# Stepping the mixer's side jobs at every eighth weight tile, not every fourth, with up to six convolution steps a visit

## The chip, the cores and the metric

The kernel runs on one core of a Trainium2 chip. Its engines are TensorE (PE), VectorE (DVE), ScalarE (ACT), GpSimd (POOL) and SyncE (SP), which here issues the transfers. Each engine executes its own list of instructions in order and waits on semaphores for the others. The metric is the device time of one execution in microseconds.

## The reference

One inference step of a two-layer decoder, for a prompt of 256 tokens and eight samples of four tokens each: 288 columns in all, 1024 features. A layer, cut to what matters:

```python
x = x + 0.5 * swiglu(rmsnorm(x, g_ffn1), w_ffn1_up, w_ffn1_down)
u = rmsnorm(x, g_mix)
x_pool, qkv, z, a, b, glu_in, gates = split(u @ w_in)
o_pool = multiscale_pool(st_pool, x_pool)                    # branch "pool"
o_dn = gated_deltanet(st_dnconv, st_dn, qkv, z, a, b)        # branch "dn"
o_cm = conformer_conv(st_cm, glu_in)                         # branch "cm": causal convolution of width 31
br = einsum('blnc,ncd->blnd', stack([o_pool, o_dn, o_cm]), w_branch)
merged = sum(sigmoid(gates) * br)
x = x + merged @ w_out
x = x + 0.5 * swiglu(rmsnorm(x, g_ffn2), w_ffn2_up, w_ffn2_down)
x = x + sigmoid(rmsnorm(x, g_ple) @ w_ple_gate) * (p[i] @ w_ple_proj)
```

The outputs are x after a last RMSNorm, and the new states of the three branches.

## The kernel before

Activations lie with the features on the 128 partitions and the 288 columns along the free axis. All large products go through one stream of weight tiles of 128x128, 1716 tiles a layer, in the order of `tile_order` (line 54). Eight tiles make a unit of 512 KB, which SP loads (`raw`); ACT rounds it to `hi` and DVE forms the rest `lo` (`prep`, line 302), two units ahead of use (`AHEAD`). A tile costs three matmuls of 288 columns (`mm3`): hi by the rounded activations, hi by their rest, lo by the rounded. `gemm` (line 331) walks over the tiles of one output; its results lie in `m` tiles in PSUM, those of side matmuls in `a` tiles.

A layer's stages, by weight tile: feed-forward 1 (0 to 527), the mixer (528 to 1107), feed-forward 2 (1108 to 1635), the embedding (1636 to 1715). The mixer's products come in the order k, glu, q, v, pool, z (528 to 751), a first gate and four `pool_w` tiles (752 to 763), gates and branch product of "pool" (to 851), the gates of "dn" (852 to 915) and "cm" (916 to 979), the branch product of "cm" (980 to 1011) and of "dn" (1012 to 1043), and `w_out` (1044 to 1107).

What the branches compute beside these products is cut into steps of generators, the side jobs: `pre` (logits, decays and norms of the delta rule), `conv` (short convolution of q, k, v), `gp` (the delta rule of the prompt: inverses, values, states, 40 steps, with `finish` for each half of it, which norms and gates the output and rounds it into `oh` and `ol`), `pool` (pooling, 4 steps), `gs` (the delta rule of the samples, 26 steps, the last eight of which multiply a mask into a 96x512 tile, run one wide matmul and update four 128x128 states), and `cm` (the width-31 convolution, 77 steps). A step issues work on DVE, ACT and PE; jobs wait for each other by flags (`gp` for `pre`'s `ready`, `gs` for an inverse of `gp`).

After every `HOOK`-th weight tile `gemm` calls the hook. In the mixer and behind it that is `pump` (line 1081). It reckons with planned costs: `te.t` is what PE was given since the last visit, `v.t` what DVE was given, and `owed` their difference, saved up to 1.5 (`CARRY`):

```python
for s in list(sides):
    for _ in range(LIMS[s[0]]):
        if self.v.t >= self.te.t + owed[0] or not step(s):
            break
```

The jobs are visited in the order pre, conv, gp, pool, gs, cm (`ORDER`), each up to its number in `LIMS`. Where a branch's result must be there, the program calls `until` (line 1089), which steps the named jobs until it is, with no weight tiles between: `get_pool` ahead of tile 760, `get_cm` ahead of 980, `get_dn` ahead of 1012 (it wants all three `finish` of the delta rule done; it names conv, pre, gp and gs).

The recorded program is then ordered by a scheduler that can shift instructions a little where their inputs are thought to be late; the order on each engine is fixed before the run.

Of the kernel before, what the change touches and what calls it, by code (L numbers as in the profile page):

```python
# [155 lines left out]
MF = (7, 4)  # L156
MP = (6, 6)
WARM = 16
HOOK = 4
WB = 3  # L160
A00 = 0
CAHEAD = 2
CTAPS = range(3, 31, 3)
DMIN = 0.0
ORDER = ("pre", "conv", "gp", "pool", "gs", "cm")
LIMS = (1, 1, 1, 1, 1, 3)


def pause(n):
# [57 lines left out]
class Net:  # L227
# [103 lines left out]
    def gemm(self, xs, nk, nout=1, spare=False, mid=None):  # L331
        pss = [self.aps()[:, :N] if spare else self.mps() for _ in range(nout)]
        for k in range(nk):
            xh, xl = xs(k)
            for ps in pss:
                self.mm3(ps, xh, xl, k == 0, k == nk - 1)
                self.tick += 1
                if self.hook and self.tick % HOOK == 0:
                    self.hook()
# [722 lines left out]
    def mix(self, l):  # L1062
# [11 lines left out]
        def step(s):  # L1074
            try:
                return next(s[1]) != "wait"
            except StopIteration:
                sides.remove(s)
                return False

        def pump():
            owed[0] = min(owed[0] + self.te.t - self.v.t, CARRY)
            self.v.t = self.te.t = 0.0
# [3 lines that stand above are left out]
# [431 lines left out]
```

## Time and profile before

| what | before |
|---|---|
| median of 3 runs | 1501.1 us (1499.58 to 3540.52) |
| profiled execution | 1498.33 us |
| its span | 1496.5 us |
| PE busy | 1482.9 us, 99% |
| DVE busy | 1077.9 us, 72% |
| ACT busy | 787.1 us, 53% |
| DMA | 250.03 MB, mean 167 GB/s |

The span is from the first to the last instruction of the program on the core. PE is busy nearly throughout; what matters is what it is busy with, and whether a stage takes more than its weight tiles need.

### The profile page before, as it was taken

The page shows a single profiled execution, that of the slowest core. Times are in us where ns is not written, and L with a number is a line of the kernel's source. Part 1 is how long each engine was busy: PE and PEld are TensorE (multiplying, and loading weights), DVE is VectorE, ACT ScalarE, POOL GpSimd, SP SyncE. Part 2 cuts the span into 40 slices and gives each one's busy share as a digit, 9 for nine tenths or more (in the row PEclk, how much of TensorE's full clock was granted, in tenths as well). Part 3 has the DMA queues.
Part 4 walks back from the last instruction along what each step waited for, and adds up shares of the span by engine and source line. Part 5 has one row for each costly group of instructions (what it writes and reads, how often), then busy time and mean ns, then how long its engine had stood idle before and what let it go on. Part 6 is the DMA issues. An engine that isn't in the chain of part 4 may idle for free.

```text
span 1496.5 us, 30281 instructions
## 1 busy us (share of the span) xinstructions
PE 1482.9 (99%) x12280; PEld 1464.2 (98%) x12280; DVE 1077.9 (72%) x2045; ACT 787.1 (53%) x1410; POOL 9.0 (1%) x34
## 2 busy tenths in 40 slices
PE   9999999999999999999999999999999999999997
PEld 9999999999999999999999999999989999999997
DVE  6575559998889655555867655699987986556556
ACT  6444446865664544443544444479557554444444
POOL 0000000000000000000000000000000000000000
PEclk9999999999999999999999999999999999999999
DMA  7555564655365555555555555555544755555552
GB/s 253 184 160 166 169 183 153 160 165 184 110 207 184 161 165 169 169 167 167 157 165 177 166 169 161 182 163 154 170 157 128 228 170 158 169 161 173 169 159 71
DMA packets 84572, 250.03 MB, mean 167 GB/s; under 512 B 19760, under 2 KB 24240, under 8 KB 84432
## 3 DMA queue, kind: packets, MB, share of 16 engines
q1 hardware_dynamic: 84000, 247.70, 53.9%
q8 instruction: 96, 1.57, 0.4%
q10 hardware_dynamic: 432, 0.40, 0.1%
q14 instruction: 44, 0.36, 0.1%
HBM read 239.52 MB, written 8.54 MB: 166 GB/s over the span
## 4 chain that ended last, share of the span: by engine, by line
PE 92%; ACT 4%; DVE 3%; issue 1%; DMA 0%; SPq 0%; DVEq 0%
PE m L205 84%; PE a L205 8%; ACT hi L310 1%; DVE lo L205 1%; DVE w L205 1%; ACT L568 0%; ACT w L716 0%; DMA x<-in_x 0%; DVE rsq L205 0%; ACT w L561 0%; ACT big L568 0%; ACT big L465 0%; DVE big L205 0%; ACT w L516 0%; ACT L701 0%
## 5 line engine op out<-in xcount | busy, mean ns | idle before, releaser
L205 PE MATMUL m<-big,hi 128*128 128x288 f32 x4008 | 803.0, 296 | 0.1
L205 DVE TENSOR_TENSOR lo<-raw,hi 128x1024 fp32r<-128x1024 f32 (+1 forms) x431 | 524.6, 1218 | 258.6 <-ACT hi L310 256.8
L310 ACT ACTIVATE hi<-raw 128x1024 fp32r<-128x1024 f32 (+1 forms) x431 | 456.3, 1059 | 452.3 <-PE m L205 274.4
L205 PEld LDWEIGHTS m<-big,hi 128*128 128x128 f32 x4008 | 643.1, 188 | 0.8 <-ACT big L346 0.3
L205 PE MATMUL m<-big,lo 128*128 128x288 f32 x2004 | 591.2, 295 | 0.0
L205 PE MATMUL m<-act,hi 128*128 128x288 f32 x2688 | 546.0, 298 | 0.6 <-ACT hi L310 0.6
L205 PEld LDWEIGHTS m<-act,hi 128*128 128x128 f32 x2688 | 430.4, 188 | 2.9 <-issue 1.2
L205 PE MATMUL m<-act,lo 128*128 128x288 f32 x1344 | 396.5, 296 | 0.5 <-DVE lo L205 0.3
L205 PEld LDWEIGHTS m<-big,lo 128*128 128x128 f32 x2004 | 377.2, 188 | 0.0
L205 PEld LDWEIGHTS m<-act,lo 128*128 128x128 f32 x1344 | 252.5, 188 | 1.8 <-DVE lo L205 1.5
L205 DVE TENSOR_TENSOR ar<-m,rsb 128x288 f32<-128x288 f32 x130 | 59.0, 454 | 47.1 <-PE m L205 43.5
L346 ACT ACTIVATE big<-h 128x288 fp32r<-128x288 f32 x96 | 41.8, 436 | 60.4 <-DVE h L205 60.4
L439 ACT ACTIVATE s<-ar 128x288 f32<-128x288 f32 x88 | 38.2, 436 | 65.5 <-DVE ar L205 65.4
L205 DVE SCALAR_TENSOR_TENSOR big<-big,par,big 128x256 f32<-128x256 f32 x160 | 70.8, 477 | 0.6
L205 DVE TENSOR_TENSOR big<-h,big 128x288 fp32r<-128x288 f32 x96 | 43.5, 454 | 19.5 <-ACT big L346 19.4
L205 DVE TENSOR_TENSOR h<-s,m 128x288 f32<-128x288 f32 x84 | 37.8, 450 | 19.3 <-ACT s L439 19.3
L371 ACT ACTIVATE sq<-x 128x288 f32<-128x288 f32 x62 | 26.9, 437 | 36.7 <-DVE x L205 36.4
L205 DVE TENSOR_TENSOR acc<-acc,sq 128x288 f32<-128x288 f32 x68 | 30.8, 454 | 11.4 <-ACT sq L371 10.9
L516 ACT ACTIVATE w<-big,par 128x256 f32<-128x256 f32 x80 | 37.2, 514 | 0.2
L205 DVE SCALAR_TENSOR_TENSOR w<-big,par,w 128x312 f32<-128x312 f32 x72 | 34.4, 533 | 2.8 <-ACT w L561 2.6
L205 DVE TENSOR_TENSOR big<-big,w 128x512 f32<-128x512 f32 x40 | 27.3, 683 | 5.6 <-ACT w L516 5.2
L205 PE MATMUL a<-w,big 32*32 32x32 f32 (+3 forms) x480 | 27.4, 223 | 0.3
(222 smaller groups left out, 893.8 us busy)
## 6 DMA issues: line engine op xcount, KB each, us to landing
raw<-in_w SPq DMA_DIRECT2D x427, 512.0 KB, 3.5
big<-in_dn_in SPq DMA_DIRECT2D x16, 512.0 KB, 5.5
out_dn_s<-big SPq DMA_DIRECT2D x8, 512.0 KB, 3.5
x<-in_x SPq DMA_DIRECT2D x4, 288.0 KB, 4.9
big<-in_cm_in SPq DMA_DIRECT2D x2, 544.0 KB, 4.6
big<-in_cm_in SPq DMA_DIRECT2D x4, 272.0 KB, 4.9
out_cm_s<-big SPq DMA_DIRECT2D x4, 272.0 KB, 4.6
raw<-in_w SPq DMA_DIRECT2D x4, 256.0 KB, 5.1
```

Source lines behind the costliest of these rows:

```text
L205: return f(*a, **k)
L310: nc.scalar.activation(hi[:, a:b], src[:, a:b], AF.Copy)
L346: nc.scalar.activation(hi, src, AF.Copy, scale=1.0 if scale is None else scale)
L371: nc.scalar.activation(s, src, AF.Square)
L439: nc.scalar.activation(s, ar, AF.Silu)
L516: nc.scalar.activation(ahead[nxt][:, i], ext[j][:, nxt:nxt + NP], AF.Copy, scale=wj(j, nxt))
```

## The change

Two constants: the hook is called after every eighth weight tile, and `cm` may take up to six steps at a visit. The other jobs keep one step a visit, and `CARRY` stays 1.5.

```diff
-HOOK = 4
+HOOK = 8
...
-LIMS = (1, 1, 1, 1, 1, 3)
+LIMS = (1, 1, 1, 1, 1, 6)
```

No instruction is added or removed on PE, DVE, POOL and SP; ACT gets 17 table loads and not 13. What moves is the order. Three places follow.

PE in layer 0 at the start of the `dn` branch product (tile 1012). `m_934` and `m_882` are the last tiles of the `cm` branch product, `m_939` and `m_937` the first of `dn`; `big_825` and `big_889` are `oh`. Before:

```order
L205 MATMUL m_934_5994<-big_803_5286,hi_922_5921 128x288
L205 MATMUL m_934_5994<-big_804_5287,hi_922_5921 128x288
L205 MATMUL m_934_5994<-big_803_5286,lo_923_5922 128x288
L205 MATMUL m_939_6016<-big_825_5388,hi_922_5921 128x288
L205 MATMUL m_943_6036<-big_825_5388,hi_929_5959 128x288
```

And in the changed kernel, where the `a` rows of 128x512 belong to the samples' state updates (`gs`) and the others to `gp` and to the samples' `finish` (its transpose is `a_888`):

```order
L205 MATMUL m_882_5786<-big_790_5192,lo_867_5693 128x288
L205 MATMUL a_886_5805<-w2_878_5762,big_545_3502 128x128 x4
L205 MATMUL a_888_5812<-cst_87,w2_860_5668 128x128
L205 MATMUL a_893_5823<-w2_877_5760,big_661_4184 128x128 x4
L205 MATMUL a_897_5834<-w2_896_5832,big_832_5492 128x512
L205 MATMUL a_898_5840<-w2_887_5810,big_387_2519 128x128 x4
L205 MATMUL a_901_5850<-w2_900_5848,big_832_5492 128x512
L205 MATMUL a_902_5856<-w2_887_5810,big_385_2517 128x128 x4
L205 MATMUL a_906_5868<-w2_905_5866,big_832_5492 128x512
...
L205 MATMUL a_928_5959<-w2_927_5957,big_832_5492 128x512
L205 MATMUL a_929_5965<-w2_925_5950,big_673_4273 128x128 x4
L205 MATMUL a_935_5996<-cst_87,w2_934_5994 128x128 x4
L205 MATMUL m_937_6005<-big_889_5814,hi_866_5692 128x288
```

Seventeen rows of side matmuls stand between `m_882` and `m_937` (six of them left out here); before, the same side matmuls stand among the weight tiles of the gates of "cm" and of the `cm` branch product. In layer 1 it is thirteen rows.

DVE at the same work. `w2_861`, `w2_868`, `w2_876` are products of `gs` for its wide matmuls, `big_848`, `big_867` the states, `lo` the rests of weight units. Before:

```order
L205 TENSOR_TENSOR w2_861_5567<-big_767_5105,cst_87 96x512
L205 TENSOR_TENSOR w2_868_5610<-big_767_5105,cst_87 96x512
L205 SCALAR_TENSOR_TENSOR big_848_5487<-big_848_5487,eg_499_3170,a_862_5569 128x128 x4
L205 SCALAR_TENSOR_TENSOR big_867_5608<-big_867_5608,eg_499_3170,a_869_5612 128x128 x4
L205 SCALAR_TENSOR_TENSOR w2_875_5655<-a_874_5650,par_85,big_584_3750 128x512
L205 TENSOR_TENSOR w2_876_5659<-big_767_5105,cst_87 96x512
L205 TENSOR_TENSOR lo_880_5670<-raw_878_5667,hi_879_5669 128x1024
L205 TENSOR_TENSOR big_826_5389<-w2_875_5655,big_825_5388 128x4x128
L205 SCALAR_TENSOR_TENSOR big_867_5608<-big_867_5608,eg_499_3170,a_877_5661 128x128 x4
L205 TENSOR_TENSOR w2_886_5714<-big_767_5105,cst_87 96x512
L205 TENSOR_TENSOR lo_890_5725<-raw_888_5722,hi_889_5724 128x1024
```

In the changed kernel (`h_892` belongs to the last group of the `cm` branch product):

```order
L205 SCALAR_TENSOR_TENSOR h_892_5820<-big_776_5086,m_882_5786 128x288
L205 TENSOR_TENSOR big_680_4306<-big_680_4306,h_892_5820 128x288
L205 SCALAR_TENSOR_TENSOR w2_891_5816<-a_888_5812,par_85,big_577_3723 128x128
L205 TENSOR_TENSOR w2_896_5832<-big_832_5492,cst_87 96x512
L205 TENSOR_TENSOR big_890_5815<-w2_891_5816,big_889_5814 128x4x32
L205 TENSOR_TENSOR w2_899_5845<-a_898_5840,egc_507_3242 128x512
L205 TENSOR_TENSOR w2_900_5848<-big_832_5492,cst_87 96x512
L205 TENSOR_TENSOR w2_899_5845<-big_554_3561,w2_899_5845 128x512
L205 SCALAR_TENSOR_TENSOR big_895_5830<-big_895_5830,eg_508_3244,a_897_5834 128x128 x4
L205 SCALAR_TENSOR_TENSOR big_895_5830<-big_895_5830,eg_508_3244,a_901_5850 128x128 x4
L205 TENSOR_TENSOR w2_903_5861<-a_902_5856,egc_507_3242 128x512
L205 TENSOR_TENSOR w2_905_5866<-big_832_5492,cst_87 96x512
```

The splits of weight units have gone from between: from `lo_885` to `lo_944` stand 58 rows of side work and of branch products, and the splits come again behind the last `finish`.

PE at the four `pool_w` tiles of layer 0 (760 to 763; the third and fourth are `m_637` and `m_638` before and `m_632` and `m_633` after). Before, `a_644` to `a_665` are 14 matmuls of `gp`:

```order
L205 MATMUL m_637_4008<-big_583_3749,hi_613_3898 128x288
L205 MATMUL m_637_4008<-big_582_3748,lo_614_3899 128x288
L205 MATMUL a_644_4065<-big_387_2519,big_384_2516 128x128
L205 MATMUL a_644_4065<-big_385_2517,big_384_2516 128x128
...
L205 MATMUL a_665_4203<-big_385_2517,big_384_2516 128x128
L205 MATMUL m_638_4014<-big_582_3748,hi_613_3898 128x288
L205 MATMUL m_639_4020<-act_403_2608,hi_613_3898 128x288
L205 MATMUL m_639_4020<-act_405_2610,hi_613_3898 128x288
```

In the changed kernel:

```order
L205 MATMUL m_631_3979<-big_575_3721,lo_607_3873 128x288
L205 MATMUL a_648_4095<-cst_87,bro_594_3819 128x128 x4
L205 MATMUL a_653_4136<-cst_87,bro_594_3819 128x128 x4
L205 MATMUL a_660_4181<-cst_87,bro_594_3819 128x128
L205 MATMUL m_632_3985<-big_575_3721,hi_606_3872 128x288
L205 MATMUL m_632_3985<-big_576_3722,hi_606_3872 128x288
L205 MATMUL m_632_3985<-big_575_3721,lo_607_3873 128x288
L205 MATMUL m_633_3991<-big_575_3721,hi_606_3872 128x288
L205 MATMUL m_634_3997<-act_403_2608,hi_606_3872 128x288
L205 MATMUL m_633_3991<-big_576_3722,hi_606_3872 128x288
L205 MATMUL m_633_3991<-big_575_3721,lo_607_3873 128x288
```

Between the pool tiles now stand nine transposes of `pre`; the matmuls of `gp` come from tile 804 on. In layer 1 it is the same.

## Rows read from the trace of the kernel before

**Rows 1.** The page: span, busy time by engine, chain that ended last by line.
```profile
span 1496.5 us, 30281 instructions
...
PE 1482.9 (99%) x12280; PEld 1464.2 (98%) x12280; DVE 1077.9 (72%) x2045; ACT 787.1 (53%) x1410; POOL 9.0 (1%) x34
...
PE m L205 84%; PE a L205 8%; ACT hi L310 1%; DVE lo L205 1%; DVE w L205 1%; ACT L568 0%; ACT w L716 0%; DMA x<-in_x 0%; DVE rsq L205 0%; ACT w L561 0%; ACT big L568 0%; ACT big L465 0%; DVE big L205 0%; ACT w L516 0%; ACT L701 0%
```

**Rows 2.** Chain in order of time (start us, us, what): a feed-forward stretch.
```profile
514.64 201.47 PE m L205 x1515
```

**Rows 3.** Stretches of layer 0's mixer; columns in the first line; sum over all eight stages.
```profile
core 0: us, PE busy (x) PEld busy (x) DVE busy (x) ACT busy (x) POOL busy (x), PEclk, DMA share, GB/s
...
447.80:462.10 14.30, 14.30 (x110) 14.10 (x109) 13.37 (x38) 6.04 (x12) 0.00 (x0) 1.00 0.67 220
462.10:474.90 12.80, 12.80 (x99) 12.80 (x98) 12.80 (x29) 6.33 (x9) 0.00 (x0) 1.00 0.51 156
...
sum 280.90, PE 279.80 PEld 271.56 DVE 250.24 ACT 177.07 POOL 3.25; mean PE 34.97 PEld 33.94 DVE 31.28 ACT 22.13 POOL 0.41
```

**Rows 4.** Timeline of DVE (start us, us, engine line op out<-in xcount [idle before]).
```profile
421.23 0.68 DVE L205 TENSOR_TENSOR w<-big,cst 96x512 fp32r<-96x512 f32 x1
421.83 1.11 DVE L205 SCALAR_TENSOR_TENSOR big<-big,eg,a 128x128 f32<-128x128 f32 x4
422.86 0.68 DVE L205 TENSOR_TENSOR w<-big,w 128x512 f32<-128x512 f32 x1
423.46 1.11 DVE L205 SCALAR_TENSOR_TENSOR big<-big,eg,a 128x128 f32<-128x128 f32 x4
...
429.88 0.16 DVE L205 TENSOR_TENSOR rsq<-f 128x4 f32<-128x4 f32 x1
430.08 0.16 DVE L205 SCALAR_TENSOR_TENSOR rsq<-rsq,ms 128x4 f32<-128x4 f32 x1
```

**Rows 5.** Timeline of PE: one wide and four narrow; transposes; a group of four.
```profile
439.46 1.29 PE L205 MATMUL a<-w,big 96*128 96x512 f32 x9
440.51 0.38 PE L205 MATMUL m<-act,hi 128*128 128x288 f32 x1
...
459.30 0.63 PE L205 MATMUL a<-cst,w 128*128 128x128 f32 x4
459.76 1.06 PE L205 MATMUL a<-w,big 128*128 128x128 f32 x8
460.58 0.38 PE L205 MATMUL m<-big,hi 128*128 128x288 f32 x1
```

**Rows 6.** Timeline of ACT: rounding to hi, squares of a finish.
```profile
438.37 0.62 ACT L346 ACTIVATE big<-w 128x512 fp32r<-128x512 f32 x1
...
447.01 0.29 ACT L889 ACTIVATE w<-w 128x128 f32<-128x128 f32 x1
...
447.43 0.31 ACT L889 ACTIVATE w<-w 128x128 f32<-128x128 f32 x1
```

**Rows 7.** Timeline of PE at the pool tiles.
```profile
324.73 3.29 PE L205 MATMUL a<-big,big 128*128 128x128 f32 x28
328.15 0.40 PE L205 MATMUL m<-big,hi 128*128 128x288 f32 x1
```

**Rows 8.** Groups by line: a table load of ACT.
```profile
L568 ACT ACT_TABLE_LOAD x5 | 6.4, 1283 | 0.1
```

**Rows 9.** Stretches at the kernel's end (columns as in rows 3).
```profile
1488.00:1490.00 2.00, 0.26 (x3) 0.00 (x0) 1.75 (x8) 0.59 (x2) 0.00 (x0) 1.00 0.00 0
1490.00:1492.00 2.00, 0.00 (x0) 0.00 (x0) 1.40 (x3) 1.22 (x3) 0.00 (x0) 1.00 0.53 198
1492.00:1494.00 2.00, 0.00 (x0) 0.00 (x0) 0.00 (x0) 0.00 (x0) 0.00 (x0) 0.60 1.01 286
1494.00:1496.50 2.50, 0.00 (x0) 0.00 (x0) 0.00 (x0) 0.00 (x0) 0.00 (x0) 0.50 0.22 85
```

## Prediction

> **What bounds the kernel now.** I read the page first, then the chain in order of time, then the mixer's stages in a table by stretches, and last the timelines of PE, DVE and ACT where the side jobs end.
>
> The page has the profiled execution: a span of 1496.5 us (1498.33 us with what lies around it), PE busy for 99% of it, and a chain that is PE work for 92%: weight matmuls 84%, matmuls into the `a` tiles 8% [rows 1]. So PE sets the time, and a change matters where PE has to wait in its own order. Outside the mixer PE runs through: 1515 weight matmuls in 201.47 us, 0.133 us each [rows 2], 0.40 us a weight tile and 3.2 us for eight.
>
> The mixer of layer 0 runs from 219.6 to 500.5 us (borders are the starts of a stage's first weight matmul, counted through the timeline): 280.9 us [rows 3] for 580 tiles, which at 0.40 would take 231.4. The excess of 49.5 us is side matmuls and waiting. The side's own part follows from the chain: 8% of the span is 120 us; 252 of those `a` matmuls are ordinary weights that use a spare buffer (42 tiles a layer, by `spare=` in `ffn` and `ple`), 34 us; the rest is 86 us, 43 a layer. So PE idles or loses about 6 us in a mixer. That is all that steadier side jobs could give back.
>
> DVE is busy for 250 of those 281 us; it is full where the last branch product runs (12.80 of 12.80 us), and yet PE takes 12.80 us there for 32 tiles, no wait at all [rows 3]. The reason is that all side jobs are done by then.
>
> **What the change does to the order.** `HOOK` 8 halves the visits (276 to 138 in a layer). At a visit `gp` and `gs` get one step each, however much budget is left, and only `cm` got a larger limit; and `CARRY` caps what is saved up at 1.5. Stepping through `pump`'s rule, before: `gp` has 40 steps and `gs` 26, and both are through when the program comes to `until` at tile 1012 of layer 0, ahead of the `dn` branch product. After: `gp` starts at tile 804 and not 752, and at tile 1012 it has 13 steps left and `gs` 8. `until` then emits them all with no weight tile between. The recorded order in the section on the change agrees: 17 groups of side matmuls in a row on PE, then `m_937`, which needs the last of their results. PE executes in that order, so it waits for the whole chain.
>
> **The price of the burst, layer 0**, from start-to-start times in the timeline of DVE before [rows 4], with the last visit's two steps counted in:
> - 8 products 96x512 at 0.60 (421.23 to 421.83): 4.8
> - 8 groups of four state updates at 1.03 (421.83 to 422.86): 8.2
> - 10 further 512-wide operations of `gp` (two for R, two for oq, one normalising, one gating, one split in each of two `finish`) at 0.60 (422.86 to 423.46): 6.0
> - 28 tiny dependent ones of two `finish` at 0.20 (429.88 to 430.08): 5.6
> - two 128-wide ones of the samples' `finish` about 0.5, and two of the previous branch product that stand ahead, 0.9.
>
> Sum 26.0 us of DVE. On top come times at which DVE has nothing else in order: the four squares of the second `finish` on ACT at 0.42 (1.7), the transposes on PE (0.5), the rounding to `oh` on ACT (0.6) [rows 5, 6], most of S1's way through PE, ACT and PE (0.8 + 0.6 + 0.8, less what DVE does meanwhile: 1.3), and handoffs between them, together about 5. The burst is 31 us long. PE's own work in it was there before too: six groups of four at 0.82, eight wide matmuls at 0.23 (439.46 to 440.51 holds one wide and one group: 1.05 less 0.82), two sets of transposes at 0.46 [rows 5]: 7.7 us. So PE newly idles for 23 us. Bounds: without any wait 26.0 - 7.7 = 18; with 4 us more (the four state loads stand behind four weight loads in SP's queue) 27.
>
> **Layer 1.** 1716 tiles a layer are no multiple of 8, so visits fall four tiles differently and 11 `gp` and 6 `gs` steps are left. Seven products 4.2, seven groups 7.2, 10 wide 6.0, tiny 5.6, a weight split that lands inside 1.1, 0.9: 25.0, waits 4.5, less PE's 4 x 0.82 + 7 x 0.23 + 0.9 = 5.8: 24 us. **Both: 47** (36 to 54).
>
> What is late next: the weights. Two and a half units of eight tiles are prepared when the burst begins, 20 tiles or 8 us for PE after it; the next `lo` follows the first group of four tiles, so nothing more is late. Weight loads are not late either: they stand ahead of the state loads.
>
> **The pool step.** The last `pool` step is now emitted at tile 760 itself, eight tiles (3.2 us) later, right ahead of `get_pool`, whose four tiles need it. Before, that wait was there too, but covered: from 324.73 to 328.15 us PE did 14 matmuls of `gp`, 28 records [rows 7]. These are not yet due after, and nine transposes (about 1.0 us) stand there instead. 3.4 + 3.2 - 1.0 = 5.6 us would be open; DVE has up to 2.5 us less to do just ahead, since `pre`'s last products and `gp`'s first come later. I take 4 a layer (1 to 6): **8**.
>
> **The clock.** At the kernel's end the granted clock is still 1.00 in 1490 to 1492 us, falls to 0.60 in the next 2 us and then to 0.50, the lower level; PE had been idle since about 1488.3 [rows 9]. In the burst PE idles for 5 to 6 us twice (the first `finish` on DVE; the second with its squares). So it may come out of the burst at 1.2 GHz: eight tiles would then take 3.2 us longer. I take 1.5 a layer (0 to 3): **3**.
>
> The Trainium skill's page "TensorE: Matmul & The Clock Gate" (Part 1, "HAM oscillation") states that idle stretches of PE send its clock back to half rate and that each return is paid for; it speaks against any change that makes a hole in PE's stream. The kernel's end agrees that an idle PE loses its clock; no row of before shows what the return costs.
>
> **Small.** Four more table loads stand in ACT's order (17 for 13), 1.283 us each [rows 8], two in each mixer. They are hidden where ACT has slack; I take 1 a layer (0 to 2.6): **2**. Given back: side matmuls come every eight tiles and wait less for DVE; half of the 6 us idle, **-6** in all (0 to -12). The number of places where side matmuls break the weight stream stays (46 and 48 before, 44 and 44 after), so nothing is saved on switching. `cm` ends at tile 932 and not 908, still ahead of 980, where it is wanted: nothing.
>
> **Sum:** 1498.3 + 47 + 8 + 3 + 2 - 6 = 1552 us. The profiled execution is 0.2% under the median of the runs shown, 1501.1, so the sum holds for either.
>
> **Rivals.**
> - *DVE covers its waits.* If no handoff shows, the bursts cost 36, and with the pool's 8 and -12 given back the time is about 1530. For it: DVE has seldom nothing to do in the recorded order. Against it: the second `finish` is a chain with nothing beside it.
> - *The clock stays low.* Half clock in both bursts and for some 16 tiles behind them, 4 + 6.4 us each in place of 1.5: 1498.3 + 47 + 21 + 8 + 2 - 3 = 1573. For it: the two holes in each burst, and the fall at the kernel's end [rows 9]. Against it: side matmuls keep some activity between. [...]
> - *Not slower.* DVE bounds the mixer (250 of 281 us), so holding back 26 us of its work until tile 1012 lets PE reach that tile earlier by as much, and the burst only gathers what PE waited for in small pieces: about 1500. It decides when PE's losses ahead of tile 1012 are 23 us a layer. The sum above finds about 6, and the last stage before `dn` shows PE at 14.30 of 14.30 us busy [rows 3]; little room.
> - *Gain.* All 12 us back and the bursts hidden would be 1486, within 2% still; nothing here reaches 1471.
>
> **Chances.** Forecast (1535 to 1565) 0.66; covered waits 0.15; low clock 0.10; not slower 0.05; a gain or something unseen 0.04. 2% is about what a measurement of this kernel can tell from no change. Against 1501.1 that is 1531: the covered case lies on it and is halved. Slower 0.85, same 0.13, faster 0.02. The range reaches from 1527 (low bounds of burst and pool, all idle time given back) to 1574.
>
> **What would show it.** In the profile after, PE's busy share in the mixers falls by some 23 us each at one place, with `m` weight matmuls ended by DVE or ACT waits; the 12.8 us ahead of the `w_out` stage stay; a stretch of 31 us with about 8 us of PE and 25 of DVE; a hole of about 4 us near the pool's four tiles; feed-forward stages unchanged. I am wrong if the `dn` product starts without a long hole, if the hole is as short as `gp`'s part alone (12 us), or if PE's losses ahead of it shrink by more than 6 us.

## The result, and the profile after

The changed kernel takes 1570.7 us against 1500.1 us for the kernel before on the same chip: a ratio of 1.0476, with an interval of 1.0464 to 1.0488. The interval is that of the undisturbed runs alone, among which the one run of 3540.52 us does not count. The forecast was slower, 1552 us with a range from 1527 to 1574; 1570.7 lies within the range, but above the 1535 to 1565 to which the forecast gave a chance of 0.66. The sign, and the place and the cause of the larger part, were as said; of the 70.6 us the forecast had 52, and what it lacks lies outside the burst.

The page of the profile after, to be held against [rows 1]: the span; busy time by engine; and the chain that ended last, by engine.

```profile
span 1569.2 us, 30266 instructions
...
PE 1507.2 (96%) x12280; PEld 1481.6 (94%) x12280; DVE 1086.3 (69%) x2045; ACT 795.1 (51%) x1414; POOL 8.9 (1%) x34
...
PE 89%; DVE 6%; ACT 3%; DMA 1%; issue 1%; SPq 0%; DVEq 0%; ACTq 0%
```

PE has the same 12280 matmuls and is busy for 24.3 us more: the same work at a lower clock, as the stretches will show. The chain, which was PE's for 92%, is so for 89%, and DVE has 6% of it. PE's waits in the mixer of layer 0 (who waits for whom, us in total, times, longest us), of the kernel before in the first row, which is all that the view has, and after in the two largest:

```profile
PE a L205 <- issue: 0.4, 1, 0.4
```

```profile
PE a L205 <- DVE w L205: 17.8, 7, 6.1
PE m L205 <- ACT big L346: 6.0, 3, 3.9
```

All rows together are 0.4 us before and 25.4 after; in layer 1 they are 1.7 and 25.9.

By stages (borders are the starts of a stage's first weight matmul, counted through the timeline of each kernel), in us:

| Stages | layer 0 before | change | layer 1 before | change | both |
|---|---|---|---|---|---|
| k, glu, q, v | 71.6 | -0.5 | 71.3 | -0.5 | -1.0 |
| pool, z, first gate and pool tiles | 37.5 | +3.2 | 36.0 | +5.9 | +9.1 |
| branch "pool", gates of dn, gates of cm | 119.2 | -4.2 | 121.1 | -6.7 | -10.9 |
| branch cm, with what `until` emits behind it | 14.3 | +35.1 | 14.7 | +33.9 | +69.0 |
| branch dn | 12.8 | +2.1 | 12.8 | +2.1 | +4.3 |
| `w_out`, feed-forward 2 | 237.5 | +1.3 | 237.4 | +0.9 | +2.2 |

That is the whole difference of the two spans, 72.7 us; the other stages moved by 0.3 us or less. The stretches of layer 0 after, as in [rows 3], with columns PE, PEld, DVE, ACT, POOL busy (and instructions), granted clock, DMA share and GB/s. The first row is the whole mixer, then the stage pool, the gates of cm, the branch cm, the branch dn, and the burst alone:

```profile
219.40:536.40 317.00, 291.16 (x2664) 279.45 (x2664) 253.90 (x584) 182.13 (x400) 3.19 (x6) 0.94 0.47 147
...
290.40:306.20 15.80, 15.11 (x113) 14.37 (x112) 11.61 (x19) 14.86 (x56) 0.00 (x0) 1.00 0.40 105
...
406.60:446.10 39.50, 38.95 (x486) 35.82 (x485) 20.77 (x48) 24.53 (x51) 1.13 (x3) 1.00 0.35 108
446.10:495.60 49.50, 30.18 (x180) 26.52 (x179) 38.14 (x116) 16.43 (x46) 0.00 (x0) 0.74 0.39 138
495.60:510.50 14.90, 14.90 (x97) 14.90 (x98) 11.10 (x23) 6.39 (x10) 0.00 (x0) 0.85 0.30 82
...
460.80:495.60 34.80, 15.48 (x67) 11.82 (x66) 26.09 (x83) 7.50 (x26) 0.00 (x0) 0.62 0.36 136
```

Two things are to be seen. First the burst: 34.8 us long, with 26.1 us of DVE, where the working had counted 26.0, and 15.5 us of PE, twice the 7.7 it had counted. Second, DVE over the whole mixer: 253.9 us busy, against 250.2 before [rows 3]. The mixer grew by 36 us and DVE's work by 4; the rest is DVE standing idle, 63 us against 31. It idles where it was idle before the change for a few us only. These are the gates of cm and the stage pool of the kernel before, in the same columns:

```profile
413.60:447.80 34.20, 34.06 (x255) 33.13 (x254) 30.25 (x72) 20.02 (x46) 0.00 (x0) 1.00 0.59 199
...
291.20:305.40 14.20, 14.11 (x108) 13.87 (x107) 13.32 (x26) 14.20 (x55) 0.00 (x0) 1.00 0.63 179
```

In the gates of cm DVE idles 18.7 us after and 4.0 before; in the stage pool 4.2 and 0.9. So the burst is 26 us of DVE work that was held back while DVE had nothing to do, one step in 3.2 us, and that is then done where PE has nothing else.

The chain of the burst in layer 0, in order of time (start, us, what):

```profile
460.37 1.24 DVE lo L205
461.62 0.33 SPq L299
462.00 4.76 DMA big<-in_dn_in
466.79 1.99 DVE big L205 x8
468.86 1.29 DVE w L205 x2
...
470.28 0.78 PE a L205
...
472.31 0.17 DVE ms L205
...
477.30 3.18 DVE big L205 x12
...
484.55 2.34 PE a L205 x9
486.91 0.70 DVE w L205
487.64 0.41 ACT w L889 x2
...
492.98 1.10 PE a L205 x4
494.10 0.76 DVE w L205
494.88 0.64 ACT big L346
495.57 0.61 PE m L205
```

It is the list of the prediction: state updates, masks, two `finish` with tiny operations 0.20 us apart, squares on ACT, transposes, rounding, and only then a weight tile. PE's pieces in it are long: 2.34 us for the nine that took 1.29 in [rows 5].

The pool's place, in the timeline of PE (start, us, tiles, and in brackets idle time and its releaser), and the same place in stretches of 2 us:

```profile
324.75 0.40 PE L205 MATMUL m<-big,hi 128*128 128x288 f32 x1 [0.52 <-ACT big L346]
325.77 0.40 PE L205 MATMUL m<-big,hi 128*128 128x288 f32 x1 [0.63 <-DVE big L205]
...
330.24 0.61 PE L205 MATMUL m<-big,hi 128*128 128x288 f32 x1 [3.94 <-ACT big L346]
```

```profile
328.00:330.00 2.00, 0.00 (x0) 0.00 (x0) 2.00 (x9) 0.69 (x3) 0.00 (x0) 0.87 0.10 41
330.00:332.00 2.00, 1.76 (x7) 1.76 (x8) 2.00 (x7) 0.57 (x2) 0.00 (x0) 0.50 0.00 0
332.00:334.00 2.00, 2.00 (x10) 2.00 (x9) 2.00 (x6) 0.12 (x1) 0.00 (x0) 0.50 0.00 0
334.00:336.00 2.00, 2.00 (x10) 2.00 (x10) 1.82 (x5) 1.85 (x3) 0.00 (x0) 0.50 0.00 0
336.00:338.00 2.00, 2.00 (x16) 2.00 (x16) 1.78 (x4) 0.41 (x1) 0.89 (x2) 0.92 0.24 20
```

PE loses 0.67, 0.90 and 4.10 us from start to start beyond a matmul's 0.133 us: 5.7 us, and 6.1 in layer 1. Behind it PE has only weight tiles, but at 0.50 of the clock: 10 matmuls in 2 us where 18 is usual. In layer 0, 23 of them take 0.24 us in place of 0.133, 2.5 us; in layer 1 it is 18, 1.9 us. It is the same behind the burst, in stretches of 4 us:

```profile
488.00:492.00 4.00, 0.00 (x0) 0.00 (x0) 2.19 (x14) 1.25 (x7) 0.00 (x0) 0.74 0.15 59
492.00:496.00 4.00, 1.52 (x6) 1.15 (x7) 2.00 (x4) 0.63 (x1) 0.00 (x0) 0.50 0.00 0
496.00:500.00 4.00, 4.00 (x18) 4.00 (x18) 0.66 (x2) 0.67 (x1) 0.00 (x0) 0.50 0.02 4
500.00:504.00 4.00, 4.00 (x32) 4.00 (x31) 3.54 (x9) 2.15 (x4) 0.00 (x0) 0.98 0.29 69
```

Branch dn takes 14.9 us for it in place of 12.8. With that the mixer of layer 0 is accounted for: waits +25.0, weight tiles at half clock behind the two holes 2.5 + 2.1, the burst's own matmuls at half clock 15.5 - 7.7 = 7.8, together 37.4 against the 36.1 us found. In layer 1 it is 24.2 + 4.0 + 7.0 = 35.2 against 34.9.

### The profile page after: what moved, and what is told of

It reads as the page before. It is cut to its first block, busy times and chain, and to the rows that moved or that the text cites. A ratio compares the mean times of both kernels' runs of the same rounds, so it can differ in the third digit from the quotient of the medians.

```text
span 1569.2 us, 30266 instructions
## 1 busy us (share of the span) xinstructions
PE 1507.2 (96%) x12280; PEld 1481.6 (94%) x12280; DVE 1086.3 (69%) x2045; ACT 795.1 (51%) x1414; POOL 8.9 (1%) x34
## 4 chain that ended last, share of the span: by engine, by line
PE 89%; DVE 6%; ACT 3%; DMA 1%; issue 1%; SPq 0%; DVEq 0%; ACTq 0%
PE m L205 81%; PE a L205 8%; DVE w L205 2%; DVE big L205 1%; DVE lo L205 1%; ACT hi L310 1%; DMA big<-in_dn_in 1%; DMA big<-in_pool_in 0%; DVE rsq L205 0%; DMA x<-in_x 0%; ACT w L716 0%; DVE h L205 0%; DVE f L205 0%; ACT w L889 0%; ACT w L516 0%
## 5 line engine op out<-in xcount | busy, mean ns | idle before, releaser
L205 PE MATMUL m<-big,hi 128*128 128x288 f32 x4008 | 809.1, 297 | 13.7 <-ACT big L346 12.5
L205 PEld LDWEIGHTS m<-big,hi 128*128 128x128 f32 x4008 | 646.4, 189 | 16.1 <-ACT big L346 14.3
L205 PEld LDWEIGHTS m<-act,lo 128*128 128x128 f32 x1344 | 253.9, 189 | 2.6 <-DVE lo L205 2.2
L205 PE MATMUL a<-w,big 32*32 32x32 f32 (+3 forms) x480 | 36.1, 246 | 23.7 <-DVE w L205 23.7
L205 PEld LDWEIGHTS a<-w,big 32*32 32x32 f32 (+3 forms) x480 | 28.7, 146 | 30.5 <-issue 21.9
L371 ACT ACTIVATE sq<-x 128x288 f32<-128x288 f32 x62 | 26.9, 436 | 32.8 <-DVE x L205 32.4
L205 DVE SCALAR_TENSOR_TENSOR w<-big,par,w 128x312 f32<-128x312 f32 x72 | 34.9, 534 | 1.7 <-ACT w L561 1.4
```

The lines of the kernel that those rows point to most:

```text
L205: return f(*a, **k)
L371: nc.scalar.activation(s, src, AF.Square)
```

## The experiments

Every kernel is the changed one with the edit shown, so `HOOK` is 8 and cm's limit 6 unless the edit says otherwise. How many steps are left at tile 1012 follows from the planner's rule, as in the prediction. Theory A is the prediction's: the price is the work left at tile 1012. The rival B is that side work in lumps of eight tiles costs PE wherever it stands.

**Limits of two for gp and gs.**

```
-LIMS = (1, 1, 1, 1, 1, 6)
+LIMS = (1, 1, 2, 1, 2, 6)
```

> The changed kernel with limits of two for gp and gs (HOOK 8 stays): by the planner's rule both jobs are through at tile 980, so nothing is left for tile 1012. Theory A (the loss is the work left over at tile 1012, emitted with no weight tile between): the stages cm.b and dn.b go back from 49.4 + 14.9 and 48.6 + 15.0 us to about 14.5 + 13 each, the 8 us at the pool's four tiles stay, the side matmuls of the burst (7.7 and 5.8 us) come back into the stages ahead: 1570.7 - 74 + 13.5 = 1510, 1503 to 1518. Theory B (lumps of side work every eight tiles cost PE time wherever they stand; the burst only gathers it): the same work now waits in lumps between tiles 800 and 980, 15 us a layer or more: 1530 to 1550.

1522.6 us, ratio 1.0158 (1.0141 to 1.0175). Neither: the branch cm is 19.3 and 13.3 us long and dn 12.8 in both layers, so the burst is gone, and 48 us with it. But 24 us stay. By stages, both layers: +9.5 at pool, z and the pool tiles, as in the changed kernel, +12.5 from branch "pool" to the gates of cm, +3.5 in branch cm. The largest wait is that at the pool tiles, 3.9 us at a time, in both layers.

**Limit of two for gp alone.**

```
-LIMS = (1, 1, 1, 1, 1, 6)
+LIMS = (1, 1, 2, 1, 1, 6)
```

> Limit of two for gp alone. By the planner's rule gp ends at tile 972 and with it goes what until waits for, so the state updates of gs that are left (8 groups of four) are stepped at later visits, up to tile 1148, and not in a burst. Theory A: no hole at tile 1012, time about that of the run with both limits, 1505 to 1520; the groups of four appear in the w_out and ffn2 stages (0.8 us each). Theory B: 1530 to 1550, as there. A third, that gs is what makes the burst long by itself: would not show here, since gs is not waited for.

1520.3 us, 1.0140 (1.0125 to 1.0155). The burst is gone here too (branch cm 13.6 and 13.3), with gs's updates spread over `w_out` and feed-forward 2, which cost 2.5 us together. It lies at the upper edge of A's figure, 1520; the same 9 us at the pool's place and 13 from there to the gates of cm remain.

**Limit of two for gs alone.**

```
-LIMS = (1, 1, 1, 1, 1, 6)
+LIMS = (1, 1, 1, 1, 2, 6)
```

> Limit of two for gs alone: gs is through at tile 980 (layer 1: 964), and at tile 1012 only the 13 (11) steps of gp are emitted in one piece. Theory A with the prediction's sums for gp's part: 10 wide at 0.60, 28 tiny at 0.20, 0.9 of the branch: 12.5 us of DVE, and the waits of its chain, which nothing covers now (squares 1.7, transposes 1, rounding 0.6, S1 and handoffs 3 to 4): 19 us long, against 34.8 in the changed kernel; gs's eight groups go back ahead of it, 7 us a layer. Time 1570.7 - 2 x 16 + 2 x 7 = 1553 (1542 to 1560). If DVE throughput alone were the price (no waits in gp's chain), the burst would be 12.5 us: 1538. If gs's updates were free in the burst (hidden behind gp's chain), the time would stay at 1570 or rise by the 14 us that moved ahead.

1548.2 us, 1.0327 (1.0311 to 1.0342), inside theory A's range and outside those of the other two. With gp's 13 steps alone the burst is 23.0 us (19 expected). Its stretch:

```profile
461.20:484.20 23.00, 11.24 (x65) 10.42 (x64) 12.68 (x41) 7.44 (x26) 0.00 (x0) 0.64 0.13 43
```

DVE has 12.7 us of work in it, as counted (12.5), and idles for 10.3: gp's chain, not DVE's throughput, sets this part. gs's steps add 11.8 us of length for 13.4 us of DVE work, so gs covers little of the chain and is nearly paid in full.

**cm's limit back to three, with HOOK 8.**

```
-LIMS = (1, 1, 1, 1, 1, 6)
+LIMS = (1, 1, 1, 1, 1, 3)
```

> HOOK 8 with cm's limit left at three, as before the change. By the planner's rule the steps of gp and gs left at tile 1012 are the same 13 + 8 and 11 + 6, only cm ends at tile 964 and not 932. Theory: the larger limit of cm is worth nothing, 1571 within 4 us. Rival: with limit six cm takes budget in the stages ahead and pushes PE into waits there (the cm gates took 39.5 us in the changed kernel against 34.2); then three is faster by 5 us or more.

1569.0 us, 1.0467 (1.0452 to 1.0483): as the changed kernel within the interval. The larger limit of cm brings nothing with HOOK 8.

**cm's limit of six, with HOOK 4.**

```
-HOOK = 8
+HOOK = 4
```

> The limit of six for cm alone, HOOK 4 as before. By the planner's rule gp ends at tile 1008 and 996, gs at 984 and 980, cm at 896: nothing is left at tile 1012. Theory (the whole price comes from HOOK): as the kernel before, 1500 within 4 us. Rival: cm's larger limit crowds out gp and makes PE wait in the stages from pool+b to cm.b: 1505 to 1515.

1503.5 us, 1.0028 (1.0018 to 1.0038). Slightly slower, 4 us and measurably so: nearly the theory's upper edge, under the rival's range. So of the two numbers that were changed, `HOOK` carries the price.

**Idle matmuls in both holes.**

```
 def until(cond, keys):
+    if not cond():
+        ps = self.mps()
+        wh = self.units[self.cur_t // UT][0]
     while not cond():
...
+                v0 = self.v.t
+                ok.append(step(s))
+                for _ in range(3 + int(4 * (self.v.t - v0))):
+                    nc.tensor.matmul(ps, wh[:, :P], wh[:, P:P + N], start=True, stop=True)
...
     until(lambda: "pool" in m, "pool")
+    for _ in range(24):
+        nc.tensor.matmul(ps, wh[:, :P], wh[:, P:P + N], start=True, stop=True)
```

> The changed kernel with idle matmuls that nothing reads (128x128 by 128x288, into a spare m tile): three and four more for each us of DVE work behind every step that until emits at tile 1012, and 24 ahead of the pool's four tiles. They keep PE working in its two holes of each layer; the side steps and the waits stay. Theory (the half clock is a price of its own: behind the pool's hole the weight matmuls run at 0.24 us for some 25 of them, behind the burst for 19, and the burst's own side matmuls take twice their time): pool+b shorter by 2.8 us, dn.b back from 14.9 to 12.8, cm.b shorter by 1 to 4 a layer: 1570.7 - 2 x 7 = 1557, 1550 to 1562. Rival: the clock is not what costs there, the waits on DVE are, and the fill only delays the chain: 1568 to 1585.

1571.4 us, 1.0476 (1.0458 to 1.0493): the theory's 14 us did not come. The stretches of layer 0 show that the clock was held, at the pool's wait and in most of the burst, but not in its last hole:

```profile
328.00:330.00 2.00, 0.36 (x4) 0.12 (x2) 2.00 (x8) 1.59 (x5) 0.00 (x0) 1.00 0.20 80
330.00:332.00 2.00, 1.58 (x12) 1.58 (x13) 2.00 (x7) 0.58 (x2) 0.00 (x0) 1.00 0.00 0
332.00:334.00 2.00, 2.00 (x18) 2.00 (x17) 1.74 (x5) 1.34 (x2) 0.00 (x0) 1.00 0.00 0
488.00:492.00 4.00, 0.46 (x3) 0.49 (x4) 2.91 (x15) 0.00 (x0) 0.00 (x0) 0.68 0.00 0
492.00:496.00 4.00, 2.49 (x11) 2.09 (x11) 1.44 (x2) 0.63 (x1) 0.00 (x0) 0.50 0.02 4
```

The branch "pool" of layer 0 is 2.3 us shorter than in the changed kernel, and 1.5 us shorter than in the run with the state loads ahead below, which has the changed kernel's order up to there; the slow tiles were 2.5 us. In layer 1 the wait at the pool tiles still brought the clock down, and the stage got back 0.9 us. The burst at full clock is no shorter: +1.0 and -1.2 us. The idle matmuls stand ahead of the side matmuls in PE's order and may have taken back what the clock gave; the run does not tell the two apart. Layer 1's stage pool also took 2.7 us longer than in the changed kernel, with one wait of 2.33 us ahead of tile 716. The chain there leads to a load of the pool's state: ACT waits 2.54 us for it, where it waits 0.72 in the changed kernel, and the rounding of the next weights stands behind it in ACT's order:

```profile
1074.42 4.03 DMA big<-in_pool_in
1078.56 1.06 ACT hi L310
```

So the clock's price is shown behind the pool's wait of layer 0; inside the burst it stays open.

**State loads a head earlier.**

```
+        nxt = load_s(0)
         yield from self.finish(l, m, 8, 1, oq)
         for h in range(H):
-            S = load_s(h)
+            S = nxt
+            nxt = load_s(h + 1) if h + 1 < H else None
```

> The changed kernel with each state load of gs's updates issued one head earlier, the first ahead of the samples' finish, so that it has landed before tile 1012. Theory (in the burst of layer 0 the chain goes through a load that was issued at 462.00 us behind weight loads and landed at 466.76): the updates start some 3 us earlier, cm.b shorter by 2 to 4 us in each layer, 1570.7 - 6 = 1565. Rival: gp's chain or DVE's work is as long, the load only ended last by a little: 1569 to 1572.

1570.4 us, 1.0472 (1.0457 to 1.0488), not to be told from the changed kernel. The chain of the burst no longer holds a load, and its updates start 3.5 us sooner:

```profile
461.81 0.87 DVE w L205 x2
463.33 1.12 DVE big L205 x4
```

Branch cm is shorter by 0.9 and 1.3 us only, little more than other stages differ between these two kernels (up to 0.8 us). The rival holds. The reason may be that while DVE waited for the load it did gp's work, which now comes later; no run shows that by itself. A load on the chain was worth a quarter of its length at most.

**pool ahead of the other jobs.**

```
-ORDER = ("pre", "conv", "gp", "pool", "gs", "cm")
-LIMS = (1, 1, 1, 1, 1, 6)
+ORDER = ("pool", "pre", "conv", "gp", "gs", "cm")
+LIMS = (1, 1, 1, 2, 1, 6)
```

> The changed kernel with pool ahead of the others in ORDER and a limit of two for gp. By the planner's rule the last pool step is emitted at tile 752, as before the change, gp ends at tile 996 and nothing is left at tile 1012. It differs from the run with gp's limit alone (1520.3) in the pool's place. Theory: the 20 us that this run had over the kernel before lie for two thirds at the pool's four tiles (a wait of 5.7 us and 2.8 us of half clock behind it, in each layer); with the step eight tiles earlier 3 us of the wait and all of the half clock go: 1520.3 - 2 x 6 = 1508, 1503 to 1513. Rival: the wait is DVE's lag behind, whatever the step's place, since no gp matmuls cover it any more: 1517 to 1524.

1524.8 us, 1.0170 (1.0155 to 1.0185), the rival's side. Against the run with gp's limit alone the first gate with the pool tiles is 2.9 and 2.6 us shorter and branch "pool" 3.7 and 8.0, so the wait at the pool tiles did shrink, in layer 0 from 5.1 to 3.6 us, with half clock still behind it. But the gates of cm are 5.0 and 3.9 us longer, the gates of dn 7.3 in layer 1 (0.9 shorter in layer 0), branch cm 4.7 and dn 1.9 in layer 0: `gp` comes later (ending at tile 996 by the planner's rule, and at 972 in that run), and the time is lost there. Taking the step first moves the loss and does not remove it.

**Limits of two for all, CARRY 3.**

```
-CARRY = 1.5
+CARRY = 3.0
-LIMS = (1, 1, 1, 1, 1, 6)
+LIMS = (2, 2, 2, 2, 2, 6)
```

> HOOK 8 with a limit of two for every job but cm (six), and CARRY 3: a visit may again emit as many steps in eight tiles as two visits did before. By the planner's rule pre ends at tile 720, gp at 892, gs at 924, cm at 940, the last pool step is emitted at 752, and nothing is left at tile 1012. Theory C (a mixer's length is DVE's busy time, 248 to 256 us in all runs so far, and its idle time; one step of gp and gs in 3.2 us starves DVE in the stages ahead, 19 us idle in the cm gates of the changed kernel against 4, and what it didn't do there is done later, at tile 1012 or before it): with the rate restored DVE's idle time falls to the 28 to 31 us of before, 1500 to 1508. Rival (lumps: eight tiles without side matmuls and then several steps in a row make PE wait for each step's DVE work, whatever the rate): 1518 to 1526, as in the run with limits of two for gp and gs alone (1522.6).

1522.2 us, 1.0158 (1.0141 to 1.0175): the rival. The mixers are 292.9 and 293.8 us, DVE's idle time 38 us in each and not 28 to 31. Now 19 us of the loss lie in pool, z and the pool tiles, where `pre` and `gp` send two steps at a time, and 6 us in k to v; behind the pool tiles nearly none. PE's waits are 10.1 and 8.0 us, against 0.4 and 1.7 before.

**Limits of two for gp and gs with HOOK 4.**

```
-HOOK = 8
-LIMS = (1, 1, 1, 1, 1, 6)
+HOOK = 4
+LIMS = (1, 1, 2, 1, 2, 3)
```

> HOOK 4 and cm's limit of three as before, with limits of two for gp and gs. By the planner's rule gp ends at tile 896, gs at 908, cm at 976. Theory C: before, DVE idles 31 and 28 us in the mixers (5.5 and 4.2 in pool+b, 8.3 and 8.8 in the dn gates), and PE can give back at most some 6 us a layer; a higher rate takes a part of it: 1490 to 1499. Rival (steps of one job in a row wait for each other, and PE with them): 1503 to 1512.

1520.7 us, 1.0145 (1.0130 to 1.0160): the rival's sign, 9 us over its range, and theory C's "more rate is better" falls. Nor is it for the rival's reason. Branch "pool", where gp and gs now run at twice their rate, is 20.5 and 17.2 us longer and the gates of dn 11.4 and 13.9 shorter, with few waits in either. PE's waits lie elsewhere. This is the view of waits of layer 0 from 440 to 475 us, where the gates of cm end:

```profile
PE m L205 <- ACT big L346: 2.5, 1, 2.5
PE a L205 <- DVE rr L205: 2.4, 1, 2.4
```

With gp and gs first and doubled, cm comes through at tile 976 only, and its last steps, a chain of norm and rounding, stand bare ahead of tile 980: 4.9 of this layer's 8.3 us of waits, and 5.8 of 9.7 in layer 1. It is a small burst of another job at another deadline, and the clock is at 0.50 behind it.

**HOOK 6.**

```
-HOOK = 8
+HOOK = 6
```

> HOOK 6, all limits as in the changed kernel. By the planner's rule 8 gp and 5 gs steps are left at tile 1012 of layer 0 (13 and 8 with HOOK 8), 3 and 3 in layer 1 (11 and 6). Theory A and C together (each step left costs what it costs in the changed kernel: 35 us of stage cm.b for 21 steps, about 1.6 a step, and half of the 11 us a layer that HOOK 8 costs without any burst): 1500 + 21 + 10 + 11 = 1542, 1528 to 1552. Theory A alone: 1500 + 31 = 1531 or less. If the price of a burst were mainly that there is one (the clock, the chain of the last finish), layer 1 would pay nearly as much as layer 0: 1550 and more.

1530.0 us, 1.0207 (1.0192 to 1.0223): theory A alone. (The counts in the expectation have one call of gs too many, with which it ends: 12 steps are left in layer 0 and 5 in layer 1.) Branch cm is 33.4 and 23.2 us long, +19.1 and +8.5. With the changed kernel's +35.1 for 21 steps and +33.9 for 17 that is 1.6 and 1.7 us a step against 1.7 and 2.0. The price goes by what is left over, not by there being a burst. In layer 1, where the pool tiles don't wait longer than before, the whole mixer is only 5.3 us longer:

```profile
984.30:1271.00 286.70, 280.87 (x2672) 273.14 (x2672) 252.50 (x590) 177.03 (x397) 3.25 (x6) 0.99 0.52 163
...
1209.20:1232.40 23.20, 18.22 (x123) 17.10 (x122) 23.17 (x65) 8.99 (x21) 0.00 (x0) 0.93 0.56 186
```

So visits further apart cost nothing there but their burst.

**Every eight tiles up to the pool tiles, then every three.**

```
-                if self.hook and self.tick % HOOK == 0:
+                if self.hook and self.tick % (HOOK if self.cur_t % 1716 < 764 else 3) == 0:
```

> Visits every eight tiles up to tile 764 of a layer, as in the changed kernel, and every three from there on; all limits as in the changed kernel (one for gp and gs). By the planner's rule gp ends at tile 991 and 977, so nothing is left at tile 1012, and no visit emits two steps of gp or gs; the pool's last step is still emitted at tile 760, with its wait of some 5.7 us and half clock behind it. Theory D (the 22 us of the runs with limits of two are the price of two dependent steps in a row, as the run with HOOK 4 and limits of two showed; eight tiles between visits cost nothing by themselves but the burst and the pool's wait): the pool's place costs 3 to 6 us a layer as in the changed kernel, the rest is as before: 1500 + 9 = 1509, 1503 to 1514. Rival (the work not done before tile 764 makes DVE late for the whole mixer, whatever comes later): 1518 to 1525, PE waiting in the dn and cm gates. A third: the pool's wait only moves PE's waits forward, DVE catches up: 1499 to 1503.

1521.5 us, 1.0153 (1.0133 to 1.0174): the rival. There is no burst and no visit with two steps of gp or gs, and 23 us remain that come from the tiles ahead of 764. The whole mixer of layer 0, the first gate with the pool tiles, and the branch "pool":

```profile
219.60:512.00 292.40, 284.23 (x2674) 274.81 (x2673) 252.26 (x589) 181.02 (x401) 3.22 (x6) 0.99 0.51 160
319.50:331.50 12.00, 6.92 (x47) 6.23 (x46) 12.00 (x36) 6.80 (x14) 1.13 (x2) 0.93 0.48 138
331.50:375.80 44.30, 44.30 (x510) 43.68 (x510) 32.81 (x68) 18.74 (x35) 0.96 (x1) 0.94 0.43 144
```

By stages, both layers: +9.1 in pool, z and the pool tiles, as in the changed kernel; +10.6 from branch "pool" to the gates of cm, +3.0 in branch cm, +1.1 in dn. PE's waits in layer 0's whole mixer, the two largest of 8.0 us:

```profile
PE m L205 <- ACT big L346: 5.1, 3, 3.9
PE a L205 <- DVE w L205: 1.3, 2, 0.9
```

4.5 of the 5.1 stand at the pool tiles, with 0.6 more for DVE. Waits (7.6 more than before, and 7.2 in layer 1) and the slow tiles behind the pool's (2.5 and 1.3 us) are 18.6 of the 23 us; the rest is not traced to a place. The later stages are longer although PE hardly waits in them, since gp's matmuls that had filled the pool's wait [rows 7] are run there: of 28 side records at the pool's place 9 are left. In the 12.00 us of the second row DVE is busy for all 12.00: PE waits for a DVE that has idled just before, 4.3 us in the stage pool against 0.9, and that idles again behind it (32.8 of 44.3 busy). It is late, and does not catch up; that what it could do there is not yet due is my reading, not shown by a run.

So the loss is split in two; by this one run the parts add up by construction. The changed kernel less this one is 1570.7 - 1521.5 = 49.2 us for the burst, and 23 are the price of wide visits ahead of tile 764. The runs with limits of two for gp, and for gp and gs, which take the burst away and leave the pool's place, end at nearly the same, 1520 and 1523. What stays open is why the second part is lost: moving the pool step (the run with pool first) moved the loss and did not remove it, and no run starves or feeds DVE in the stage pool alone. No version was found that beats the kernel before.

## Why the prediction held in sign and missed in size

- **What bounds the kernel.** That PE sets the time and every wait in its order counts is confirmed. The "6 us" of idle PE in a mixer, made by subtraction, were not there: the view of waits has 0.4 and 1.7. (The 8% that was subtracted is a rounded figure; half a per cent of the span is 3.7 us a layer.) And I asked only what PE would lose. DVE's count says more of the result: its work is nearly the same in all these kernels (248 to 257 us a mixer), and DVE's idle time is 31 and 28 us before, 63 and 60 after. That a mixer is the sum of the two holds for any engine and shows no cause; where DVE idles shows where work was held back. I had the number, 250 of 281 [rows 3], and used it against one rival only.
- **The burst, DVE's work: 26.0 us.** Measured 26.1, and 25.3 in layer 1 for 25.0; its place and that the next weight tile waits for all of it were right. The operations of layer 0 are those of the list, one by one. That the sums agree to 0.1 us is luck: the 26.1 hold 0.8 us of a weight split that is not in the list, and the 28 tiny operations are busy for 4.6 us where 5.6 were counted from start to start. The reason given for layer 1's smaller count is wrong: after, the side matmuls stand behind the same tiles in both layers (804, 812, up to 1004 and 1012), so the visits don't fall four tiles differently there; the count was right even so, with eight groups of updates and not seven in the stretch.
- **The burst's waits: 5 us. Mis-sized.** They are 8.7 (34.8 less 26.1), and 6.9 in layer 1 (32.2 less 25.3) for 4.5. PE's pieces in the chain were priced at the durations of [rows 5], taken at full clock; in the burst they take twice that (nine in 2.34 us in place of 1.29), since the clock is down from its first hole on. The late state loads, my upper bound, were on the chain, but were worth only 1 us. Over the branch cm: +31 and +29.5 us forecast, +35.1 and +33.9 measured, 8.5 us short.
- **Net price of the burst: 47, with the clock 50.** By the runs that take it away, 48.1 (limits of two for gp and gs), 49.2 (visits of three behind the pool tiles) and 50.4 (gp's limit). This was the step the forecast stood on, and its size holds, though in part by luck: against the run with visits of three the branch cm is 66.1 us longer where 60.5 were forecast, what comes behind it 5.3 us where 3 were, and the stages from branch "pool" to the gates of cm are 21.5 us shorter where PE's 13.5 were. So the whole miss, some 19 us, lies in the terms outside the burst, which follow.
- **The pool's place: 8. Mis-sized by most.** The wait is 11.8 us for both layers where I took 4 a layer (the 5.6 us that I had worked out was the right figure; DVE's "2.5 us less to do" was not there, as it was full for the whole stage). Behind it come 4.4 us of half clock that no term had: I looked for the clock's price at the burst only. And the gp matmuls that had covered the wait are run later, in time of their own, so that the wait counts in full.
- **Given back -6, table loads 2.** The first was wrong: before, there were 2 us of waits to give back, and from branch "pool" to the gates of cm, ahead of the burst, the changed kernel is 10.9 us shorter, less than PE's own 13.5 us that went into the burst. All that lies outside the burst costs 23 us by the run with visits of eight up to tile 764; pool, table loads and the time given back made 4. No run takes out the table loads alone: the stage pool got 1.5 and 1.2 us longer, and they are not told apart there from PE's small waits.
- **The clock: 3.** Behind the burst 4.3 us, in branch dn; right in kind, and near the value. The rival "the clock stays low" at 1573 comes closest in time. Its half clock within the bursts is there; its 16 tiles at half clock behind each are 6, and the pool's place, which it priced as the forecast did, makes up for the rest. What the page "TensorE: Matmul & The Clock Gate" (Part 1, "HAM oscillation") of the Trainium skill says, that idle stretches send the clock back and each return is paid for, agrees with this trace: 0.50 behind both holes of each layer. Here it was 2.5 and 1.9 us at the pool and 2.1 at each burst.
- **Small things not foreseen.** `w_out` and feed-forward 2 got 2.2 us longer. `until` books all its work as debt in `owed`, which blocks every further step, and gp's last step, a group of four matmuls of 0.82 us, stands behind tile 1172, in feed-forward 2, in both layers.
- **"Not slower" and "covered waits"** fall: DVE idles 8.7 us in the burst, 10.3 when gp is alone. The low chances given to them stand.
- **The range.** Its upper end, 1574, is not the sum of the high bounds as they stand (54, 12, 6 and 5.2 with nothing given back make 1575.5 from 1498.3); and that it held the result is in part luck, since its width came mostly from the burst (36 to 54), and what was missing lay elsewhere.

In the runs made here the rate of the side jobs is thus bounded on both sides: one step at every eighth tile starves DVE, and two steps of gp and gs at every fourth push cm to its deadline.

## What to carry to other kernels

Where a second engine is nearly full, add up its busy and its idle time by stage, before and after: in this kernel a scheduler that is visited less often showed first as that engine idling in a stage where nothing waits, and most of the price was paid later, at a deadline. Count the steps left at each deadline from the planner's own rule, price the left-over as a chain, with the waiting engine's pieces at its low clock if it idles for several us within, and add the slow stretch behind every new hole, the small ones too. Raising one job's steps per visit moves the left-over to another job's deadline: whatever job is last there ends in a bare chain.

## What the runs showed of the hardware that was not expected

- In a hole of 4.1 us in PE's stream, with two short waits just ahead of it, the granted clock goes from 1.00 to 0.50, the lower of its two levels (1.2 GHz). PE works again without a pause from 330.24 us; the stretches up to 336 us are at 0.50, and that from 336 to 338 has 0.92. The price was 23 matmuls at 0.24 us in place of 0.133, and 18 in layer 1.
- Through the burst the clock stays low although PE works in it: 15.5 of 34.8 us busy at a mean clock of 0.62. Idle matmuls between the side steps held it at 1.00 up to 488 us, and the burst was no shorter for it; as these stand ahead of the side matmuls, the run does not say what the clock alone would be worth.
- A state load of 4.76 us in the chain of the burst gave back about 1 us of its stage when it was taken out, and the median time moved by 0.3 us. What ends a wait last need not be what sets it by much.
